# Encoder block on one core: the down projection becomes seven block products like the up projection, with its operands kept in DRAM

## The chip, the cores and the metric

The kernel runs on one NeuronCore of a Trainium2 chip. The metric is the device time of one execution in microseconds (us); lower is better. The engines are named as the profile names them: PE multiplies matrices (PEld is its weight load), DVE and ACT work elementwise, POOL does a little elementwise work at the very end, and SP issues the DMA transfers.

## What is computed

One layer of an encoder with 512 tokens and a model width of 2048; everything is float32. The change touches the last two lines of the block, the MLP:

```python
h = h + mixed @ w_out
hn = _rmsnorm(h, norm_mlp_w)
h = h + jnp.square(jax.nn.relu(hn @ w_mlp_up)) @ w_mlp_down
return _rmsnorm(h, norm_final_w)
```

`w_mlp_up` is 2048 x 8192 and `w_mlp_down` 8192 x 2048. Everything ahead of `w_out` (the input projection, neighbourhood attention, a gated delta rule, two projections) is the same in both kernels.

## The kernel before

Activations lie transposed, features on the 128 partitions and the 512 tokens along the row, so a 128-feature tile of `h` is 128x512. A float32 weight unit of 128x1024 (eight 128x128 blocks) is loaded in one 512 KB DMA and split in two: ACT rounds it to the PE's format (`wh`, the CAST of lines 89 and 94), DVE subtracts (`wl`, the TENSOR_TENSOR of lines 90 and 95). The right-hand operand is split the same way, and each block product takes three matmuls: high by high, high by low, low by high. `wh` and `wl` have three buffers each (line 87).

**Up projection (lines 841 to 964).** It runs as Winograd's form of Strassen's algorithm. A pair i of output tiles (`m0`, `m1`) and the two halves of the contraction give four weight units A11, A12, A21, A22; the tokens are cut in two halves of 256. Instead of eight products of a unit by a token half there are seven: A11, A12, A22 and the sums S1 to S4 of weight units, each against one of seven operands X11, X21, X22, T1 to T4 that are made once from `h` while `w_out` runs (lines 870 to 888). A product is 24 matmuls of 128x256 (lines 912 to 914), a pair 168, the 32 pairs 5376. A pair uses three PSUM banks a, b, c, and the results are gathered with copies and adds on ACT and DVE (lines 933 to 963): `t1`, `t5` and `u2` hold products between their uses. In program order, banks alternate: b is written by S2, then c by S1 and a by A12, then b again by S3, then c by S4, then b by A22. relu, the row scale `rB` and the square end in tiles `ur`, which are stored to `hidD` in DRAM (lines 959, 964), 64 tiles of 128x512.

**Down projection (lines 966 to 1028).** Plain: for each batch b of 2048 hidden features 16 tiles of `hidD` are reloaded (`hr`) and split whole (`hih`, `hil`, line 844). For each of the 16 output tiles two units of `w_mlp_down` are loaded and split, 48 matmuls of 128x512 run into one bank, and DVE adds the bank to `Ha`, which holds all of `h` in SBUF (line 983). Four batches make 62 such steps; the last two output tiles of the last batch run in token halves (64 times three matmuls of 128x256, lines 1016 to 1018), so that the final RMSNorm of the first half runs beside the matmuls of the second.

**What sets the order.** Each engine works through its own list in order; a scheduler sets these lists at build time. An instruction that waits holds everything behind it on its engine. `pump` (line 101) advances the RMSNorm statistics between matmuls.

Of the kernel before, what the change touches and what calls it, by code (L numbers as in the profile page):

```python
# [49 lines left out]
def tile_hybrid_block(  # L50
# [88 lines left out]
    def rstd_bcast(ps, sumsq, nm, cs=range(4), wait=0):  # L139
# [4 lines left out]
        dg = ev(f"dg_{nm}")  # L144
# [31 lines left out]
    hidD = dp.tile([64, 128, T], F32, name="hidD")  # L176
# [607 lines left out]
    with ExitStack() as p1:  # L784
# [56 lines left out]
        def load_hid(k):  # L841
            raw = ev(f"hr{k}")
            nc.sync.dma_start(out=raw, in_=hidD[k])
            return split(raw, big(f"hih{k}"), big(f"hil{k}"))
# [4 lines left out]
        def operand(src, name):  # L849
            t = bq.tile([128, T], F32R, tag="B2", name=name) if name.startswith("X11") else big(name)  # L850
            return split(src, t[:, 0:256], t[:, 256:512])

        lo_t, hi_t = slice(0, 256), slice(256, 512)
        XS = {}
        with ExitStack() as p5:
            tr = p5.enter_context(tc.tile_pool(name="tr", bufs=8, side="right", reuse_waits="tile"))
            TR = []
            xs = []
            for n, m in enumerate(m for j in range(8) for m in (j, j + 8)):
# [9 lines left out]
                xs.append(xr)  # L869
                if n % 2 == 0:  # L870
                    XS["11", m] = operand(xr[:, lo_t], f"X11_{m}")
                else:
                    j = n // 2
                    x0, x1 = xs[n - 1], xs[n]
                    XS["21", j] = operand(x1[:, lo_t], f"X21_{j}")
                    XS["22", j] = operand(x1[:, hi_t], f"X22_{j}")
                    t = tr.tile([128, 4, 256], F32, tag="tr", name=f"TR{j}")
                    V.tensor_tensor(out=t[:, 0], in0=x0[:, lo_t], in1=x0[:, hi_t], op=ALU.subtract)
                    V.scalar_tensor_tensor(out=t[:, 1], in0=t[:, 0], scalar=-1.0, in1=x1[:, hi_t], op0=ALU.mult, op1=ALU.subtract)
                    V.tensor_tensor(out=t[:, 2], in0=x1[:, hi_t], in1=x0[:, hi_t], op=ALU.subtract)  # L880
                    V.scalar_tensor_tensor(out=t[:, 3], in0=t[:, 1], scalar=-1.0, in1=x1[:, lo_t], op0=ALU.mult, op1=ALU.subtract)
                    TR.append(t)
            tasks.append(stat("h", sq))
            for o, e in (("T2", 1), ("T1", 0), ("T3", 2), ("T4", 3)):
                for j in range(8):
                    XS[o, j] = operand(TR[j][:, e], f"X{o}_{j}")

        with ExitStack() as p6:
            sm = p6.enter_context(tc.tile_pool(name="sm", bufs=1, side="right", reuse_waits="tile"))

            def load_a(src, name):
                raw = sm.tile([128, 1024], F32, tag="a", name=f"raw_{name}", bufs=2)
                nc.sync.dma_start(out=raw, in_=src)
                return raw

            def sums(name, bufs=4):
                return sm.tile([128, 1024], F32, tag="sum", name=name, bufs=bufs)

            def et(name):
                return sm.tile([128, 256], F32, tag="et", name=name, bufs=6)  # L900
# [6 lines left out]
            def product(ps, w, o, first=False):  # L907
                hi, lo = w
                for j in range(8):
                    rh, rl = XS[o, j]  # L910
                    c = slice(j * 128, (j + 1) * 128)
                    PE.matmul(ps, hi[:, c], rh, start=first and j == 0, stop=False, skip_group_check=True)  # L912
                    PE.matmul(ps, hi[:, c], rl, start=False, stop=False, skip_group_check=True)  # L913
                    PE.matmul(ps, lo[:, c], rh, start=False, stop=j == 7, skip_group_check=True)  # L914
                    if j % NPUMP == NPUMP - 1:
                        pump()

            for i in range(32):
                m0 = i // 8 * 16 + i % 8
                m1 = m0 + 8  # L920
                a11 = load_raw(wup[m0, 0], f"A11_{i}")
                a21 = load_a(wup[m1, 0], f"A21_{i}")
                a22 = load_raw(wup[m1, 1], f"A22_{i}")
                a12 = load_raw(wup[m0, 1], f"A12_{i}")
                s1, s3 = sums(f"S1_{i}"), sums(f"S3_{i}")
                V.tensor_tensor(out=s1, in0=a21, in1=a22, op=ALU.add)
                V.tensor_tensor(out=s3, in0=a21, in1=a11, op=ALU.add)
                a, b, c = (bank()[:, 0:256] for _ in range(3))
                t1, t5, u2 = et(f"t1_{i}"), et(f"t5_{i}"), et(f"u2_{i}")
                r0, r1 = ev(f"ur{m0}"), ev(f"ur{m1}")  # L930
                s2, s4 = sums(f"S2_{i}"), sums(f"S4_{i}")
                product(a, wsplit(a11, f"A11_{i}"), "11", True)
                S_.copy(out=t1, in_=a)
                V.tensor_tensor(out=s2, in0=s1, in1=a11, op=ALU.add)
                if i == 0:
                    V.tensor_tensor(out=s4, in0=s2, in1=a12, op=ALU.add)
                    product(c, wsplit(s4, f"S4_{i}"), "22", True)
                    S_.copy(out=t5, in_=c)
                    product(a, wsplit(a12, f"A12_{i}"), "21")
                product(b, wsplit(s2, f"S2_{i}"), "T2", True)  # L940
                V.tensor_tensor(out=u2, in0=b, in1=t1, op=ALU.add)
                product(c, wsplit(s1, f"S1_{i}"), "T1", i > 0)
                if i == 0:
                    V.tensor_tensor(out=t5, in0=c, in1=t5, op=ALU.subtract)
                else:
                    S_.copy(out=t5, in_=c)
                    product(a, wsplit(a12, f"A12_{i}"), "21")
                V.scalar_tensor_tensor(out=r0[:, lo_t], in0=a, scalar=0.0, in1=rB[:, lo_t], op0=ALU.max, op1=ALU.mult)
                product(b, wsplit(s3, f"S3_{i}"), "T3")
                V.tensor_tensor(out=t5, in0=b, in1=t5, op=ALU.add)  # L950
                V.tensor_tensor(out=t5, in0=t5, in1=t1, op=ALU.add)
                V.scalar_tensor_tensor(out=r1[:, hi_t], in0=t5, scalar=0.0, in1=rB[:, hi_t], op0=ALU.min, op1=ALU.mult)
                if i > 0:
                    V.tensor_tensor(out=s4, in0=s2, in1=a12, op=ALU.add)
                    product(c, wsplit(s4, f"S4_{i}"), "22")
# [31 lines left out]
        def finish(half, ts, sq):  # L987
# [4 lines left out]
            for m in range(16):  # L992
# [118 lines left out]
```

## Time and profile before

| | us |
|---|---|
| median of 3 runs (2923.11 to 2926.89) | 2926.62 |
| the profiled execution | 2922.42 |
| its span, first to last instruction | 2920.6 |
| PE busy in the span | 2850.9 |
| DVE busy | 1723.6 |
| ACT busy | 1017.2 |

The profiled execution is 4.2 us below the median. The mean granted clock of PE is 0.993 of full speed. In the page's 40 slices PE is busy over 90% in nearly all, so PE's list of matmuls is nearly the span, and a stage is read by the time between its first and last matmul. The stages that the change touches are the end of `w_out`, the up projection, which ends at 2199 us, and the down projection with the last norm.

### The profile page before, as it was taken

How to read it: one execution, taken by the hardware profiler on the slowest of the kernel's cores; microseconds unless marked ns; L12 is line 12 of the kernel's file. 1: busy time of each engine (PE TensorE's matmuls, PEld its weight loads, DVE VectorE, ACT ScalarE, POOL GpSimd, SP SyncE). 2: the span in 40 equal slices, each digit the busy share in tenths (PEclk: the TensorE clock that was granted, in tenths of full speed). 3: DMA queues.
4: the chain of work that ended last, by engine and by line, in shares of the span. 5: the costliest groups of instructions: out<-in, count | busy, mean ns of one | idle time of the engine just before them, and what ended most of it. 6: DMA issues, size and time to landing. Idle time of an engine off the chain costs nothing.

```text
span 2920.6 us, 39434 instructions
## 1 busy us (share of the span) xinstructions
PE 2850.9 (98%) x15736; PEld 2462.6 (84%) x15736; DVE 1723.6 (59%) x2592; ACT 1017.2 (35%) x1549; POOL 24.8 (1%) x66
## 2 busy tenths in 40 slices
PE   8999999999999999999996999999999999999998
PEld 6778788888788888888886999999997888888887
DVE  6888769744554444444448888888875242332333
ACT  6444322232333333222334444444444231222332
POOL 0000000000000000000000000000000000000000
PEclk9999999999999999999998999999999999999999
DMA  7655663655632323543433334333437343343332
GB/s 230 190 183 187 211 188 121 205 158 176 190 120 92 92 86 121 172 147 116 143 117 116 127 129 139 130 127 131 131 115 262 98 152 101 119 132 95 109 100 87
DMA packets 170874, 412.31 MB, mean 141 GB/s; under 512 B 34369, under 2 KB 46721, under 8 KB 170689
## 3 DMA queue, kind: packets, MB, share of 16 engines
q1 hardware_dynamic: 170016, 407.69, 43.8%
q0 software_dynamic: 672, 2.10, 0.3%
q8 instruction: 123, 2.02, 0.3%
q14 instruction: 63, 0.51, 0.1%
HBM read 350.84 MB, written 58.88 MB: 140 GB/s over the span
## 4 chain that ended last, share of the span: by engine, by line
PE 87%; DMA 6%; DVE 5%; issue 1%; ACT 1%; SPq 0%; DVEq 0%; ACTq 0%
PE ps_b L117 11%; PE ps_b L115 11%; PE ps_b L116 11%; PE ps_mm L115 9%; PE ps_mm L117 9%; PE ps_mm L116 9%; PE ps_b L912 7%; PE ps_b L913 7%; PE ps_b L914 7%; DMA bB<-rowD 1%; DMA Nd<-bB 1%; DVE wl_in L90 1%; DMA kb<-rowD 0%; DMA XQ<-Nd 0%; PE ps_ax L589 0%
## 5 line engine op out<-in xcount | busy, mean ns | idle before, releaser
L115 PE MATMUL ps_mm<-xh,wh_in 128*128 128x512 f32 x1416 | 565.9, 400 | 3.2 <-ACT wh_in L89 3.2
L117 PE MATMUL ps_mm<-xh,wl_in 128*128 128x512 f32 x1416 | 559.0, 395 | 0.7 <-DVE wl_in L90 0.7
L116 PE MATMUL ps_mm<-xl,wh_in 128*128 128x512 f32 x1416 | 558.5, 394 | 0.0
L115 PE MATMUL ps_b<-hih,wh_dn 128*128 128x512 f32 x992 | 386.6, 390 | 1.0 <-ACT hih L94 1.0
L117 PE MATMUL ps_b<-hih,wl_dn 128*128 128x512 f32 x992 | 386.0, 389 | 1.3 <-DVE wl_dn L90 1.3
L116 PE MATMUL ps_b<-hil,wh_dn 128*128 128x512 f32 x992 | 386.4, 390 | 0.0
L89 ACT CAST wh_in<-raw_in 128x1024 fp32r<-128x1024 f32 x177 | 186.0, 1051 | 408.7 <-PE ps_mm L116 331.8
L117 PEld LDWEIGHTS ps_mm<-xh,wl_in 128*128 128x128 f32 x1416 | 267.0, 189 | 60.8 <-DVE wl_in L90 1.6
L115 PEld LDWEIGHTS ps_mm<-xh,wh_in 128*128 128x128 f32 x1416 | 267.1, 189 | 58.4 <-ACT wh_in L89 3.6
L116 PEld LDWEIGHTS ps_mm<-xl,wh_in 128*128 128x128 f32 x1416 | 267.0, 189 | 54.8 <-issue 0.2
L89 ACT CAST wh_dn<-raw_dn 128x1024 fp32r<-128x1024 f32 x124 | 130.8, 1055 | 459.5 <-PE ps_b L116 446.5
L90 DVE TENSOR_TENSOR wl_dn<-raw_dn,wh_dn 128x1024 fp32r<-128x1024 f32 x124 | 151.9, 1225 | 230.3 <-ACT wh_dn L89 230.1
L90 DVE TENSOR_TENSOR wl_in<-raw_in,wh_in 128x1024 fp32r<-128x1024 f32 x177 | 216.0, 1221 | 119.8 <-ACT wh_in L89 110.2
L115 PEld LDWEIGHTS ps_b<-hih,wh_dn 128*128 128x128 f32 x992 | 186.2, 188 | 42.0 <-ACT hih L94 3.4
L116 PEld LDWEIGHTS ps_b<-hil,wh_dn 128*128 128x128 f32 x992 | 186.2, 188 | 40.9 <-DVE hil L95 2.3
L117 PEld LDWEIGHTS ps_b<-hih,wl_dn 128*128 128x128 f32 x992 | 186.2, 188 | 40.1 <-DVE wl_dn L90 2.1
L914 PE MATMUL ps_b<-XT,wl_S 128*128 128x256 f32 x768 | 217.3, 283 | 0.0
L913 PE MATMUL ps_b<-XT,wh_S 128*128 128x256 f32 x768 | 217.3, 283 | 0.0
L912 PE MATMUL ps_b<-XT,wh_S 128*128 128x256 f32 x768 | 217.2, 283 | 0.0
L94 ACT CAST wh_S<-S 128x1024 fp32r<-128x1024 f32 x128 | 134.1, 1048 | 211.7 <-PE ps_b L913 202.1
L95 DVE TENSOR_TENSOR wl_S<-S,wh_S 128x1024 fp32r<-128x1024 f32 x128 | 156.6, 1223 | 31.5 <-ACT wh_S L94 29.0
L983 DVE TENSOR_TENSOR Ha<-ps_b,Ha 128x512 f32<-128x512 f32 x62 | 42.9, 692 | 189.2 <-PE ps_b L117 189.2
(352 smaller groups left out, 5204.5 us busy)
## 6 DMA issues: line engine op xcount, KB each, us to landing
raw_in<-in_win SPq DMA_DIRECT2D x177, 512.0 KB
raw_A<-in_wup SPq DMA_DIRECT2D x128, 512.0 KB
raw_dn<-in_wdn SPq DMA_DIRECT2D x124, 512.0 KB
raw_wo<-in_wout SPq DMA_DIRECT2D x32, 512.0 KB
hidD<-ur SPq DMA_DIRECT2D x64, 256.0 KB
hr<-hidD SPq DMA_DIRECT2D x64, 256.0 KB
gD<-g SPq DMA_DIRECT2D x32, 256.0 KB
raw_pa<-in_wpa SPq DMA_DIRECT2D x16, 512.0 KB
```

The lines of the kernel that those rows point to most:

```text
L89: S_.copy(out=hi, in_=raw)
L90: V.tensor_tensor(out=lo, in0=raw, in1=hi.bitcast(F32), op=ALU.subtract)
L94: S_.copy(out=hi, in_=src)
L95: V.tensor_tensor(out=lo, in0=src, in1=hi.bitcast(F32), op=ALU.subtract)
L115: PE.matmul(ps, hi[:, w], rh, start=first and kk == 0, stop=False)
L116: PE.matmul(ps, hi[:, w], rl, start=False, stop=False)
L117: PE.matmul(ps, lo[:, w], rh, start=False, stop=last and kk == 7)
L912: PE.matmul(ps, hi[:, c], rh, start=first and j == 0, stop=False, skip_group_check=True)
L913: PE.matmul(ps, hi[:, c], rl, start=False, stop=False, skip_group_check=True)
L914: PE.matmul(ps, lo[:, c], rh, start=False, stop=j == 7, skip_group_check=True)
L983: V.tensor_tensor(out=H[m], in0=ps, in1=H[m], op=ALU.add)
```

## The change

Both projections now use one routine for the seven products. In the new order a pair goes Q4 (A22 by T4), P5 (S1 by T1), P1 (A11 by X11), P6 (S2 by T2), P7 (S3 by T3), P3 (S4 by X22), P2 (A12 by X21). Bank a takes Q4 and P2, bank c takes P5 and P3, and bank b takes P1, P6 and P7 directly after one another, P6 and P7 accumulating onto what is there; each partial sum is copied out in between (`tA`, `tB`).

The seven operands of the down projection are made from the hidden tiles at the end of each up pair, four more DVE operations, and stored to `hidD`, which is now [4 batches, 7 kinds, 128, 8, 256]. At each batch 28 loads of 256 KB bring them back through four buffers (`et`, which `tA` and `tB` use as well), and 56 splits of 128x256 fill them. `h` is no longer held in SBUF: each down pair loads its two tiles from `hTD` and stores them back, and twelve are reloaded at the end. Down work goes two pairs at a time, product by product in turn, as do the first and last two pairs of up. The first two up pairs start with P1 and P2, ahead of the splits of T1 to T4. The weight sums are made in place. The last two down pairs use another product order, and each half of the tokens is normed and stored by tiles of 128 KB.

The core of the diff (the up stage's old code and the last norm are cut):

```diff
-    hidD = dp.tile([64, 128, T], F32, name="hidD")
+    hidD = dp.tile([4, 7, 128, 8, 256], F32, name="hidD")
...
+            ROLE = {"P1": "11", "P2": "21", "P3": "22", "Q4": "T4", "P5": "T1", "P6": "T2", "P7": "T3"}
+            BANK = {"P1": "b", "P6": "b", "P7": "b", "P5": "c", "P3": "c", "Q4": "a", "P2": "a"}
+            FIRST = {"P1", "P5", "Q4", "P2"}
+            ORDER = ("Q4", "P5", "P1", "P6", "P7", "P3", "P2")
...
+                elif q == "P1":
+                    S_.copy(out=tA[:, 1], in_=ps)
+                elif q == "P6":
+                    S_.copy(out=tB[:, 1], in_=ps)
+                elif q == "P7":
+                    add(r1[:, hi_t], ps, tB[:, 0])
+                    add(r1[:, lo_t], ps, tA[:, 0])
+                    V.scalar_tensor_tensor(out=r1, in0=r1, scalar=0.0, in1=rB, op0=ALU.min, op1=ALU.mult)
+                    S_.activation(out=r1, in_=r1, func=AF.Square)
...
+                nc.sync.dma_start(out=hidD[b, 0, :, j, :], in_=r0[:, lo_t])
+                nc.sync.dma_start(out=hidD[b, 1:3, :, j, :].rearrange("o p t -> p o t"), in_=r1.rearrange("p (o t) -> p o t", o=2))
+                add(tA[:, 0], r0[:, lo_t], r0[:, hi_t], ALU.subtract)
+                V.scalar_tensor_tensor(out=tA[:, 1], in0=tA[:, 0], scalar=-1.0, in1=r1[:, hi_t], op0=ALU.mult, op1=ALU.subtract)
+                V.scalar_tensor_tensor(out=tB[:, 0], in0=tA[:, 1], scalar=-1.0, in1=r1[:, lo_t], op0=ALU.mult, op1=ALU.subtract)
+                add(r0[:, hi_t], r1[:, hi_t], r0[:, hi_t], ALU.subtract)
+                nc.sync.dma_start(out=hidD[b, 4:6, :, j, :].rearrange("o p t -> p o t"), in_=tA)
+                nc.sync.dma_start(out=hidD[b, 3, :, j, :], in_=tB[:, 0])
+                nc.sync.dma_start(out=hidD[b, 6, :, j, :], in_=r0[:, hi_t])
...
+            def a_tile(name):
+                return sm.tile([128, 1024], F32, tag="a", name=name, bufs=7)
+
+            def et(name):
+                return sm.tile([128, 2, 256], F32, tag="et", name=name, bufs=4)
...
+            up_group((0, 1), ("P1", "P2", "Q4", "P5", "P6", "P7", "P3"), first)
+            for i in range(2, 30):
+                up_group((i,), ORDER)
+            up_group((30, 31), ORDER)
+
+            NB = 4
+            def operands(b):
+                operand_tiles(OPS, f"h{b}_")
+                for o in ("T4", "T1", "11", "T2", "T3", "22", "21"):
+                    for j in range(0, 8, 2):
+                        raw = et(f"hr{b}{o}{j}")
+                        nc.sync.dma_start(out=raw, in_=hidD[b, OPS.index(o), :, j : j + 2, :])
+                        for e in range(2):
+                            fill(o, j + e, raw[:, e])
...
+                for q in order:
+                    for i, p in zip(idx, ps):
+                        t = run_product(p, q, a_tile)
+                        h0, h1 = p.h0, p.h1
+                        if q == "Q4":
+                            add(h1[:, lo_t], h1[:, lo_t], t, ALU.subtract)
...
+            for b in range(NB):
+                operands(b)
+                for g in range(0, 8, 2):
+                    if b < NB - 1 or g < 6:
+                        down_group(b, (g, g + 1), ORDER, lambda i, p, q, b=b: store(b, i, p, q))
...
+            down_group(NB - 1, (6, 7), ("Q4", "P1", "P6", "P7", "P2", "P5", "P3"), collect)
...
-                for u in range(2):
-                    unit_mm(ps, load_unit(wdn[m, 2 * b + u], f"dn{b}_{m}_{u}"), hid, 8 * u, u == 0, u == 1)
-                V.tensor_tensor(out=H[m], in0=ps, in1=H[m], op=ALU.add)
```

Three places show how the lists move. First PE in an up pair, number 10 of 32. Before, where one product gives way to the next (`ps_b` with its number is a bank; XT3_0 is block 0 of T3):

```order
L914 MATMUL ps_b_14542<-X21_7_12039,wl_A12_10_14641 128x256
L912 MATMUL ps_b_14543<-XT3_0_12098,wh_S3_10_14669 128x256
L913 MATMUL ps_b_14543<-XT3_0_12098,wh_S3_10_14669 128x256
L914 MATMUL ps_b_14543<-XT3_0_12098,wl_S3_10_14670 128x256
L912 MATMUL ps_b_14543<-XT3_1_12101,wh_S3_10_14669 128x256
```

The same pair after, at the hand-over of bank 14612 from P6 (S2) to P7 (S3):

```order
L904 MATMUL ps_b_14612<-XT2_x7_12069,wl_S2_u10_14640 128x256
L902 MATMUL ps_b_14582<-X22_x0_10855,wh_S4_u10_14702 128x256
L903 MATMUL ps_b_14582<-X22_x0_10855,wh_S4_u10_14702 128x256
L904 MATMUL ps_b_14582<-X22_x0_10855,wl_S4_u10_14703 128x256
L902 MATMUL ps_b_14582<-X22_x1_10856,wh_S4_u10_14702 128x256
L903 MATMUL ps_b_14582<-X22_x1_10856,wh_S4_u10_14702 128x256
L902 MATMUL ps_b_14612<-XT3_x0_12070,wh_S3_u10_14669 128x256
L903 MATMUL ps_b_14612<-XT3_x0_12070,wh_S3_u10_14669 128x256
```

Before, the bank of S3 was last written 48 matmuls earlier. Now five matmuls of S4 (11 in every second pair) stand between two products in one bank. Between P1 and P6 no other matmul stands. Then ACT at the same pair. Before:

```order
L94 CAST wh_A12_10_14640<-raw_A12_10_14536 128x1024
L933 COPY t1_10_14545<-ps_b_14542 128x256
L94 CAST wh_S3_10_14669<-S3_10_14539 128x1024
L94 CAST wh_S4_10_14701<-S4_10_14551 128x1024
L946 COPY t5_10_14546<-ps_b_14544 128x256
L94 CAST wh_A22_10_14733<-raw_A22_10_14534 128x1024
```

After:

```order
L94 CAST wh_S2_u10_14639<-A22_u10_14539 128x1024
L94 CAST wh_S3_u10_14669<-A21_u10_14540 128x1024
L979 COPY tA_u10_14572<-ps_b_14612 128x256
L94 CAST wh_S4_u10_14702<-A22_u10_14539 128x1024
L94 CAST wh_A12_u10_14731<-raw_A12_u10_14537 128x1024
L981 COPY tB_u10_14573<-ps_b_14612 128x256
```

The copy of line 981, which P7 waits for, stands behind the cast of A12, and this cast takes the `wh` buffer of S2, which P6 reads. Last, DVE at the change to batch 1 of the down projection. Before (`Ha` is `h`, dn1_11_0 a unit of batch 1):

```order
L90 TENSOR_TENSOR wl_dn1_11_0_21592<-raw_dn1_11_0_21589,wh_dn1_11_0_21591 128x1024
L90 TENSOR_TENSOR wl_dn1_11_1_21622<-raw_dn1_11_1_21619,wh_dn1_11_1_21621 128x1024
L983 TENSOR_TENSOR Ha_19801<-ps_b_21526,Ha_19801 128x512
L90 TENSOR_TENSOR wl_dn1_12_0_21654<-raw_dn1_12_0_21651,wh_dn1_12_0_21653 128x1024
L90 TENSOR_TENSOR wl_dn1_12_1_21684<-raw_dn1_12_1_21681,wh_dn1_12_1_21683 128x1024
```

After, from the split of S1 of the first pair (d1_0) to the weight sum A22 + A21 of the second (d1_1):

```order
L95 TENSOR_TENSOR wl_S1_d1_0_22061<-A22_d1_0_21979,wh_S1_d1_0_22060 128x1024
L95 TENSOR_TENSOR X22_h1_0_21767<-hr1220_21927,X22_h1_0_21767 128x256
L95 TENSOR_TENSOR X22_h1_1_21768<-hr1220_21927,X22_h1_1_21768 128x256
L95 TENSOR_TENSOR X22_h1_2_21769<-hr1222_21933,X22_h1_2_21769 128x256
L95 TENSOR_TENSOR X22_h1_3_21770<-hr1222_21933,X22_h1_3_21770 128x256
L95 TENSOR_TENSOR X22_h1_4_21771<-hr1224_21939,X22_h1_4_21771 128x256
L95 TENSOR_TENSOR X22_h1_5_21772<-hr1224_21939,X22_h1_5_21772 128x256
L95 TENSOR_TENSOR X22_h1_6_21773<-hr1226_21945,X22_h1_6_21773 128x256
L95 TENSOR_TENSOR X22_h1_7_21774<-hr1226_21945,X22_h1_7_21774 128x256
L909 TENSOR_TENSOR h1_3_21993<-h1_3_21993,ps_b_22033 128x256
L909 TENSOR_TENSOR A22_d1_1_21987<-A22_d1_1_21987,A21_d1_1_21988 128x1024
```

Eight splits of X22, and behind the last row shown the eight of X21, stand ahead of the second pair's S1 split, though their products come five and six places later in the order.

## Rows read from the trace of the kernel before

**Rows 1.** The page: busy time by engine; the chain that ended last by engine.

```profile
PE 2850.9 (98%) x15736; PEld 2462.6 (84%) x15736; DVE 1723.6 (59%) x2592; ACT 1017.2 (35%) x1549; POOL 24.8 (1%) x66
...
PE 87%; DMA 6%; DVE 5%; issue 1%; ACT 1%; SPq 0%; DVEq 0%; ACTq 0%
```

**Rows 2.** Windows, us: span, busy by engine (count), clock, DMA share, GB/s.

```profile
1535.00:1557.00 22.00, 1.65 (x5) 1.13 (x5) 17.23 (x39) 9.73 (x26) 0.00 (x0) 0.50 0.28 95
1557.00:1577.00 20.00, 20.00 (x157) 19.36 (x156) 16.48 (x20) 7.70 (x10) 0.00 (x0) 0.95 0.38 120
1600.00:1800.00 200.00, 200.00 (x1672) 200.00 (x1671) 167.22 (x200) 90.17 (x109) 0.00 (x0) 1.00 0.40 131
2195.00:2230.00 35.00, 33.27 (x154) 24.59 (x153) 19.79 (x28) 14.85 (x22) 0.00 (x0) 1.00 0.90 309
2300.00:2500.00 200.00, 200.00 (x884) 165.62 (x883) 67.52 (x72) 48.54 (x53) 0.00 (x0) 1.00 0.38 119
```

**Rows 3.** Groups, 1600:1800: line, engine, tiles, count, busy us, mean ns, idle.

```profile
L95 DVE TENSOR_TENSOR wl_S<-S,wh_S 128x1024 fp32r<-128x1024 f32 x40 | 48.9, 1223 | 9.4 <-ACT wh_S L94 8.6
...
L94 ACT CAST wh_S<-S 128x1024 fp32r<-128x1024 f32 x40 | 41.9, 1048 | 64.4 <-PE ps_b L913 64.4
...
L950 DVE TENSOR_TENSOR t<-ps_b,t 128x256 f32<-128x256 f32 x10 | 4.2, 425 | 6.9 <-PE ps_b L914 6.9
```

**Rows 4.** Timeline of DVE in the down projection: start, us, what [idle before].

```profile
2444.56 0.69 DVE L983 TENSOR_TENSOR Ha<-ps_b,Ha 128x512 f32<-128x512 f32 x1 [3.35 <-PE ps_b L117]
...
2455.44 0.69 DVE L983 TENSOR_TENSOR Ha<-ps_b,Ha 128x512 f32<-128x512 f32 x1 [3.35 <-PE ps_b L117]
```

**Rows 5.** Groups of the down projection, 2200:2920.

```profile
L983 DVE TENSOR_TENSOR Ha<-ps_b,Ha 128x512 f32<-128x512 f32 x62 | 42.9, 692 | 189.2 <-PE ps_b L117 189.2
...
L1018 PE MATMUL ps_b<-hih,wll 128*128 128x256 f32 x64 | 18.1, 283 | 0.0
```

**Rows 6.** Timeline, end of an up product and the add that reads it.

```profile
1696.14 0.28 PE L914 MATMUL ps_b<-XT,wl_A 128*128 128x256 f32 x1
...
1696.46 0.42 DVE L961 TENSOR_TENSOR t<-ps_b,t 128x256 f32<-128x256 f32 x1 [0.69 <-PE ps_b L914]
```

**Rows 7.** Timeline, an ACT cast and the copy behind it.

```profile
1699.23 1.05 ACT L94 CAST wh_A<-raw_A 128x1024 fp32r<-128x1024 f32 x1
...
1700.19 0.37 ACT L933 COPY t<-ps_b 128x256 f32<-128x256 f32 x1
```

**Rows 8.** Timeline, from w_out to the up projection.

```profile
1526.94 0.28 PE L912 MATMUL ps_b<-X,wh_A 128*128 128x256 f32 x1
...
1527.86 0.33 SPq L866 DMA_DIRECT2D hTD<-xr  x1
...
1529.94 0.72 ACT L868 ACTIVATE xr<-xr,nlw_s 128x512 f32<-128x512 f32 x1 [1.45 <-DMA hTD<-xr]
...
1535.03 10.81 DVE L95 TENSOR_TENSOR XT<-TR,XT 128x256 fp32r<-128x256 f32 x32
...
1545.87 6.31 SPq L893 DMA_DIRECT2D raw_A<-in_wup  x3
...
1555.35 0.58 PE L912 MATMUL ps_b<-X,wh_S 128*128 128x256 f32 x1 [23.61 <-ACT wh_S L94]
```

**Rows 9.** Waits of PE, 2195:2920.

```profile
PE ps_b L117 <- DVE wl_dn L90: 1.3, 2, 0.7
```

**Rows 10.** The chain in 2195:2222: start, us, what.

```profile
2202.17 4.37 DMA hr<-hidD
...
2207.94 3.38 DMA hr<-hidD
```

**Rows 11.** Timeline of PE where down begins, 2199:2202.

```profile
2199.42 0.39 PE L115 MATMUL ps_b<-hih,wh_dn 128*128 128x512 f32 x1
```

**Rows 12.** Timeline of the end, 2903:2921.

```profile
2904.29 0.41 DVE L1021 TENSOR_TENSOR Ha<-ps_b,Ha 128x256 f32<-128x256 f32 x1
...
2910.58 3.73 DVE L996 TENSOR_TENSOR Ha<-ps_b,Ha 128x256 f32<-128x256 f32 x11 [1.72 <-ACT rB L838]
```

More of the change, by code (lines that the diff above doesn't have):

```diff
@@ L868, in tile_hybrid_block @@
                 S_.activation(out=xr, in_=xr, func=AF.Copy, scale=nlw_s[:, m : m + 1])
[L869 removed]
+                j = n // 2
                 if n % 2 == 0:
[L871 to L882 removed]
@@ L883, in tile_hybrid_block @@
[L883 to L900, printed above, removed]
+                    x0 = xr
@@ L902, in wsplit, with load_a @@
+            operand_tiles(OPS[3:], "x")
+            early_fill = [(o, j) for o in OPS[3:] for j in range(8)]
+            tr_src = {(o, j): TR[o][:, j] for o, j in early_fill}
+            def load_a(pool_tile, src):
+                nc.sync.dma_start(out=pool_tile, in_=src)
+                return pool_tile
             def wsplit(raw, name):
@@ new lines, in open_pair, with run_product @@
+            def open_pair(nm, a11, a12):
+                p = Pair()
+                p.nm, p.ps, p.step = nm, {}, 0
+                p.a11, p.a12 = a11, a12
+                p.keep = False
+                return p
+            def run_product(p, q, sums):
+                nm = p.nm
+                if q == "Q4":
+                    w = wsplit(p.a22, f"A22_{nm}")
+                elif q == "P1":
+                    w = wsplit(p.a11, f"A11_{nm}")
+                elif q == "P2":
+                    w = wsplit(p.a12, f"A12_{nm}")
+                elif q == "P5":
+                    if not p.keep:
+                        add(p.a22, p.a22, p.a21)
+                    w = wsplit(p.a22, f"S1_{nm}")
+                elif q == "P6":
+                    if p.keep:
+                        add(p.a22, p.a22, p.a21)
+                        s2 = sums(f"S2_{nm}")
+                    else:
+                        s2 = p.a22
+                    add(s2, p.a22, p.a11)
+                    p.s2 = s2
+                    w = wsplit(s2, f"S2_{nm}")
+                elif q == "P7":
+                    add(p.a21, p.a21, p.a11)
+                    w = wsplit(p.a21, f"S3_{nm}")
+                else:
+                    add(p.s2, p.s2, p.a12)
+                    w = wsplit(p.s2, f"S4_{nm}")
+                bk = BANK[q]
+                if bk not in p.ps:
+                    p.ps[bk] = bank()[:, 0:256]
+                product(p.ps[bk], w, ROLE[q], q in FIRST)
+                return p.ps[bk]
@@ new lines, in tile_hybrid_block @@
+            first = [up_open(i) for i in range(2)]
+            heads = {}
+            for i, p in enumerate(first):
+                for q in ("P1", "P2"):
+                    heads[i, q] = wsplit(p.a11 if q == "P1" else p.a12, f"{q}_u{i}") if (i, q) in ((0, "P1"), (0, "P2"), (1, "P1")) else None
+            tasks.append(stat("h", sq))
+            for o, j in early_fill[:8]:
+                fill(o, j, tr_src[o, j])
+            for i, p in enumerate(first):
+                for q in ("P1", "P2"):
+                    w = heads[i, q] or wsplit(p.a12, f"{q}_u{i}")
+                    p.ps[BANK[q]] = bank()[:, 0:256]
+                    product(p.ps[BANK[q]], w, ROLE[q], True)
```

293 lines of the change are left out of this document (177 added, 116 removed).

## Prediction, written before the changed kernel ran

> **What bounds the kernel now.** The page comes first: PE is busy 98% of the span and makes 87% of the chain that ended last [rows 1], so time is won or lost only where PE's list gets shorter or stops. The windows by stage come next [rows 2]. In the up projection PE never rests at the full clock of 2.4 GHz, and DVE is busy 167.22 of 200 us: whatever is added to DVE there has little room. In the down projection PE is busy all the time too, with DVE at 67.52 of 200. The reader should see that the change makes PE's list shorter where DVE had room to spare, and that DVE takes its place. Groups, waits and the timeline then give the prices. A change of 0.2%, about 6 us, is what a measurement of this kernel can tell from none.
>
> **Matmuls of the down projection.** Before, a step of 48 wide matmuls takes 2455.44 - 2444.56 = 10.88 us [rows 4], and there are 62 steps [rows 5]: 674.6 us. The last two tiles take 3 x 64 = 192 matmuls of 256 columns [rows 5]. One of those costs 200 / 1672 = 0.1196 us [rows 2], so 23.0 us. Together 697.6. After, 32 pairs of 168 such matmuls make 5376 x 0.1196 = 643.0. That is **-54.6 us**. It is less than an eighth of 697.6, since two of the narrow matmuls cost 0.239 us and one wide one 0.227.
>
> **Waits of down before.** Down runs from 2199.42 [rows 11] to 2904.29 [rows 12], 704.9 us, 7.3 more than its matmuls. Only 1.3 of them stand in the longest row of PE's waits [rows 9], the rest is spread over the reload of the hidden tiles. They go with the old code: **-7.3**.
>
> **Start of up.** From 1526.94 to 2199.42 up takes 672.5 us [rows 8, 11] for 643.0 of matmul: 29.5 lost, of them 23.61 in one wait [rows 8]. The rows show it: 32 splits of T1 to T4 take DVE 10.81 us, then a weight load and the sums of weights until 1555.35 [rows 8]. After, P1 and P2 of two pairs, 96 matmuls, stand ahead of the need for T4, 72 more than before: 72 x 0.1196 = 8.6 us of work under the splits. The first product behind them is Q4, which takes A22 without a sum; before, sums and their split ran from about 1549.4 (1545.87 plus the load) to 1555.35, 5.9 us. Against it, the broadcast of `rB` stands between P2 of the first pair and P1 of the second and waits for a DVE operation behind the first eight splits; that wait lies beside the splits. I take 8.6 + 5.9 + 1 = **-15.5**, with -8 and -22 as ends (no sums saved; all but the load saved).
>
> **The 28 single pairs of up.** Here work is added to the path. P1, P6 and P7 accumulate in one bank one behind another, and each next product waits until ACT has copied the sum out. The trace of before shows no such wait, so I build it from rows. An add starts 0.32 us after the start of the last matmul of its product [rows 6]; a copy of 128x256 takes 0.37 [rows 7]. P1 to P6: 0.32 + 0.37 + some 0.05 for the signal, less the 0.12 after which the next matmul would have gone: 0.62 exposed, with nothing in between. P6 to P7: the copy stands behind the cast of A12, and this waits for P6 to give up a `wh` buffer, as casts of sums do now [rows 3]. Cast and copy stand 1700.19 - 1699.23 = 0.96 apart [rows 7]. So 0.16 + 0.96 + 0.37 + 0.05 - 0.12 = 1.42, of which five or eleven matmuls of S4 cover 0.60 or 1.32. On average 0.46 is left. With 0.12 for DVE, which at 17.5 us of work (16.7 now, from 167.22 in ten pairs, plus four small operations and two wider ones in the place of small ones) has little slack, the sum is 1.2 x 28 = **+34**. The ends are 0.62 x 28 = 17, if the second copy is hidden, and 2.04 x 28 = 57, if the pulled-up matmuls cover nothing. The rows of ACT's order decide for the middle.
>
> The Trainium skill, Perfetto Trace Analysis, section Matmuls, speaks against this: independent matmul groups should rotate through different PSUM banks, so that emptying one overlaps the next group. Taken by itself, the rule makes both hand-overs bubbles: +57 in place of +34.
>
> **Change from up to down.** The first loads of operands need buffers that `tA` and `tB` of pairs 30 and 31 hold until stored. After the last product of pair 30 come an add (0.42 [rows 3]), relu and square (0.7 and 0.6 as halves or wholes of such rows), and about three operations of 0.42, some 3 us; the store, 1529.94 - 1527.86 = 2.1 [rows 8]; the load, 4.37 [rows 10]; two splits, 0.7. That makes 10, of which pair 31's last product covers 2.9, and then DVE is short: a group of two pairs needs 22 operations of 1.22 [rows 3] and 16 of 0.42, 33.6 us, and the 56 splits of 10.81 / 32 = 0.34 add 18.9, 52.5 for 40.2 of matmul. So 7.5 + 12.3, **+20**. Ends: +8, if the splits find room in the groups around it; +35, if loads, at 0.90 DMA share already before [rows 2], fall behind as well.
>
> **Changes to batches 1 to 3.** The first tiles come free 5.7 us into the last group of a batch, and the last are needed 5.7 before the end of the next: 69 us, in which DVE has 33.6 x 69 / 40.2 + 18.9 = 76.6. That is 7.6 too much, and since eight splits of X22 and eight of X21 stand ahead of the second pair's S1, I take 8 each: **+24**. Ends 0 (the excess goes into slack of the groups beside) and 45 (15 each).
>
> **Clock.** Before the start of up PE was granted 0.50, its level of 1.2 GHz, during the long wait, and 0.95 in the 20 us after it, with 157 matmuls in place of 167 [rows 2]. That cost 10 x 0.12 = 1.2 us. The short waits in 2195:2230 did not lower it. For four changes I take 1.2 each: **+5**, between 0 and 10. The Trainium skill, TensorE: Matmul & The Clock Gate, last table, warns against idle gaps between bursts of matmuls, as they send the clock back to half; by that rule the term stands, by the row of 2195:2230 alone it would be 0.
>
> **End.** After the last product 2920.6 - 2904.29 = 16.3 us remain now. Then the squares of four tiles and more sums on PE lengthen the statistics, and sixteen output transfers a half take the place of four: **+3.5**, between 0 and 8. All other work keeps its cover: four more small DVE operations and five stores a pair lie beside matmuls, as do the loads and stores of `h`, at 0.38 to 0.40 of the DMA queues [rows 2]. If the DMA cover failed, it would show as waits of ACT for raw tiles.
>
> **Sum.** -54.6 - 7.3 - 15.5 + 34 + 20 + 24 + 5 + 3.5 = **+9**. Against the profiled execution of 2922.4 that is 2931.5, against the median, which lies 4.2 higher, 2935.5. I predict 2935.
>
> **Rivals.**
> - **It gets faster: cover is better than I walk.** If the second copy hides (17 for 34), the splits at the batch changes go into DVE's slack in the groups beside (0 to 8 for 24), and the first change costs its latency alone (8 to 12 for 20), the sum falls by 45, to -35: 2892. For it: in the down projection DVE has much room today [rows 2], and two interleaved pairs give each copy 2.9 us. Against: the order lists put the splits in front of the second pair's operands. It decides from the point where hand-overs, changes, clock and end together cost less than the 77.4 us gained (my walk has 86.5).
> - **DVE and loads fall further behind.** Both hand-overs exposed (57), 15 at each batch change (45), 30 at the first: +60, so 2985 at the worst; half of the way, +35, gives 2962. For it: the DMA share of 0.90 at the change [rows 2]. Against: DVE's excess, as worked out, is only 7.6.
> - **The start does not gain.** If the new head of up waits for its loads as the old one did, the -15.5 goes: +24, 2951. For it: the weight loads at 1545.87 also waited for the splits [rows 8]. Against: 8.6 us of matmuls are ready without them.
>
> **How the numbers follow.** The forecast has 0.40; of it 0.14 lies within 0.2% and 0.26 above. Faster has 0.30, of which 0.02 lies within 0.2%. The heavier loss has 0.20, all slower. The start without gain has 0.10, of which 0.04 lies within 0.2%, if other terms are kinder. So faster 0.28, same 0.20, slower 0.52. The range goes from 2898, which leaves out the lower half of the first rival, to 2964, which leaves out the worst of the second. The forecast's own range is 2924 to 2947.
>
> **What would show it.** In the profile after: up pairs 21.2 to 21.4 us apart in place of 20.1; PE waits at the first S2 matmul for the copy of line 979 (about 0.6 each) and at the first S3 matmul for that of line 981; a group of down at 40.2 us in mid-batch without waits; PE waits for DVE's `wl` or operand tiles of some 8 us at each batch change and 20 at the first; a wait of about 10 at the start in place of 23.6. I am wrong if up pairs keep 20.1, or if groups at a change keep 40.

## The result and the profile after

| | before | after |
|---|---|---|
| median, us | 2926.7 (2923.1 to 2926.9, 4 runs) | 2955.6 (2953.1 to 2963.2, 4 runs) |
| profiled execution | 2922.4 | 2953.1 |
| span | 2920.6 | 2951.3 |

The changed kernel is slower: 1.0106 of the time of before, 95% interval 1.0086 to 1.0126, or +28.9 us between the medians. The forecast was +9, or 2935, with a range of 2898 to 2964 and a range of its own of 2924 to 2947.

The page of the changed kernel, busy time and the chain by engine, answers to [rows 1]:

```profile
PE 2831.7 (96%) x17944; PEld 2547.0 (86%) x17944; DVE 2070.7 (70%) x3195; ACT 1167.5 (40%) x1869; POOL 24.8 (1%) x66
...
PE 76%; DVE 9%; DMA 8%; ACT 3%; issue 2%; SPq 0%; DVEq 0%; ACTq 0%
```

PE is busy 19 us less than before in a span that is 31 us longer: it has less work and stands more. DVE has 347 us more to do. Where PE stands is told by its waits from 1520 us to the end (waiting matmul <- releaser: us in total, times, longest):

```profile
PE ps_b L902 <- ACT wh_S_d L94: 16.2, 6, 3.5
PE ps_b L902 <- ACT tA_u L979: 13.5, 28, 1.0
PE ps_b L902 <- ACT wh_A_d L94: 9.8, 3, 3.7
PE ps_b L902 <- ACT XT_h L94: 9.1, 2, 8.3
PE ps_b L904 <- DVE wl_S_u L95: 8.4, 13, 0.7
PE ps_b L904 <- DVE wl_A_d L95: 8.1, 4, 2.7
```

Names with `_u` belong to up, with `_d` and `_h` to down. There are two kinds: 28 small waits for the copy of line 979, one for each single pair of up, with 13 for a `wl` beside them; and a few long ones in down. The windows (columns as in [rows 2]) show the stages:

```profile
1600.00:1800.00 200.00, 193.16 (x1573) 189.38 (x1572) 158.20 (x198) 89.84 (x122) 0.00 (x0) 1.00 0.45 138
2219.00:2229.00 10.00, 1.74 (x11) 1.26 (x9) 10.00 (x17) 2.90 (x5) 0.00 (x0) 0.71 0.58 168
...
2410.00:2415.00 5.00, 2.32 (x17) 2.11 (x17) 4.25 (x11) 3.07 (x7) 0.00 (x0) 0.93 0.84 257
2425.00:2430.00 5.00, 3.21 (x13) 2.92 (x14) 4.97 (x8) 2.53 (x4) 0.00 (x0) 0.50 0.76 280
2380.00:2445.00 65.00, 56.29 (x436) 55.38 (x435) 57.24 (x101) 34.62 (x66) 0.00 (x0) 0.92 0.68 224
2440.00:2480.00 40.00, 40.00 (x336) 40.00 (x335) 33.98 (x40) 14.69 (x14) 0.00 (x0) 1.00 0.52 170
```

Up ran 1672 matmuls in 200 us before [rows 2], now 1573 in the same 200. In mid-batch, 2440:2480, down runs without a gap. The change to batch 1 lies in 2380:2445: 436 matmuls, at 0.1196 us each 52.1 of 65 us, so 12.9 lost. All losses below are counted in this way, time less 0.1196 for each matmul, summed over the stretch in which matmuls come late.

| part (profiled executions, us) | forecast | measured |
|---|---|---|
| matmuls of down | -54.6 | -54.6 |
| waits of the old down | -7.3 | -7.3 |
| start of up | -15.5 | -16.9 |
| 28 single pairs | +34 | +38.8 |
| change from up to down | +20 | +26.3, of them waits 17.7 |
| changes to batches 1 to 3 | +24 | +40.0, of them waits 26.7 |
| clock | +5 | in the two rows above: about 15 of the 21.9 that are not wait |
| end | +3.5 | +2.6 |

The rows for the matmuls and the waits of the old down are worked out by count and price, the others are read from the trace. Ahead of the change the profiled execution of after was 1.5 us quicker, and 3.3 us of the span's 30.7 are in no row (delays under 0.05 us each, and the rounding of 0.1196 over 10,700 matmuls).

### The profile page after: what moved, and what is told of

Read it like the earlier page. It is cut to its first block, busy times and chain, and to the rows that moved or that the text cites. A ratio compares the mean times of both kernels' runs of the same rounds, so it can differ in the third digit from the quotient of the medians.

```text
span 2951.3 us, 45595 instructions
## 1 busy us (share of the span) xinstructions
PE 2831.7 (96%) x17944; PEld 2547.0 (86%) x17944; DVE 2070.7 (70%) x3195; ACT 1167.5 (40%) x1869; POOL 24.8 (1%) x66
## 4 chain that ended last, share of the span: by engine, by line
PE 76%; DVE 9%; DMA 8%; ACT 3%; issue 2%; SPq 0%; DVEq 0%; ACTq 0%
PE ps_b L902 12%; PE ps_b L904 11%; PE ps_b L903 11%; PE ps_mm L116 8%; PE ps_mm L115 8%; PE ps_mm L117 8%; PE ps_b L115 4%; PE ps_b L117 4%; PE ps_b L116 4%; DMA hr<-hidD 2%; ACT wh_S_u L94 1%; DMA bB<-rowD 1%; DMA Nd<-bB 1%; DVE wl_S_u L95 1%; DVE A_u L909 1%
## 5 line engine op out<-in xcount | busy, mean ns | idle before, releaser
L902 PE MATMUL ps_b<-XT_x,wh_S_u 128*128 128x256 f32 x768 | 223.2, 291 | 13.7 <-ACT tA_u L979 13.5
L902 PE MATMUL ps_b<-XT_h,wh_S_d 128*128 128x256 f32 x768 | 221.1, 288 | 12.6 <-ACT wh_S_d L94 12.6
L904 PE MATMUL ps_b<-XT_h,wl_S_d 128*128 128x256 f32 x768 | 221.0, 288 | 0.8 <-DVE wl_S_d L95 0.8
L903 PE MATMUL ps_b<-XT_h,wh_S_d 128*128 128x256 f32 x768 | 220.9, 288 | 0.0
L904 PE MATMUL ps_b<-XT_x,wl_S_u 128*128 128x256 f32 x768 | 217.6, 283 | 0.0
L903 PE MATMUL ps_b<-XT_x,wh_S_u 128*128 128x256 f32 x768 | 217.6, 283 | 0.0
L95 DVE TENSOR_TENSOR wl_S_u<-A_u,wh_S_u 128x1024 fp32r<-128x1024 f32 x128 | 155.0, 1223 | 47.9 <-ACT wh_S_u L94 47.8
L95 DVE TENSOR_TENSOR wl_S_d<-A_d,wh_S_d 128x1024 fp32r<-128x1024 f32 x124 | 151.6, 1223 | 21.9 <-ACT wh_S_d L94 21.0
L902 PEld LDWEIGHTS ps_b<-XT_x,wh_S_u 128*128 128x128 f32 x768 | 147.1, 192 | 22.7 <-ACT tA_u L979 19.2
L902 PEld LDWEIGHTS ps_b<-XT_h,wh_S_d 128*128 128x128 f32 x768 | 151.1, 197 | 13.4 <-ACT wh_S_d L94 13.4
L902 PE MATMUL ps_b<-X_h,wh_A_d 128*128 128x256 f32 x512 | 146.6, 286 | 10.3 <-ACT wh_A_d L94 9.8
L904 PEld LDWEIGHTS ps_b<-XT_h,wl_S_d 128*128 128x128 f32 x768 | 151.2, 197 | 1.0 <-DVE wl_S_d L95 1.0
```

The lines of the kernel that those rows point to most:

```text
L95: V.tensor_tensor(out=lo, in0=src, in1=hi.bitcast(F32), op=ALU.subtract)
L902: PE.matmul(ps, hi[:, c], t[:, lo_t], start=first and j == 0, stop=False, skip_group_check=True)
L903: PE.matmul(ps, hi[:, c], t[:, hi_t], start=False, stop=False, skip_group_check=True)
L904: PE.matmul(ps, lo[:, c], t[:, lo_t], start=False, stop=j == 7, skip_group_check=True)
```

## Experiments

Ratios are to runs of the kernel before on the same chip. Losses by run, in us, from the profiled execution; "up pair" is the distance of two single pairs of up. In code that no edit touches, up starts at 1525.4 us in the changed kernel's profile and at up to 1534.7 in those of the experiments (e3), so the losses, which count from up on, price an edit more closely than the difference of two medians.

| run | median, us | of before (95%) | up pair | first change | batch change, mean |
|---|---|---|---|---|---|
| changed kernel | 2955.6 | 1.0106 (1.0086 to 1.0126) | 21.5 | 26.3 | 13.3 |
| e1, up order | 2925.0 | 0.9989 (0.9979 to 1.0000) | 20.1 | 26.5 | 14.1 |
| e2, late splits | 2945.9 | 1.0062 (1.0047 to 1.0077) | 21.5 | 26.7 | 8.3 |
| e3, no reload | 2915.1 | 0.9957 (0.9940 to 0.9974) | 21.5 | 27.0 | 0.0 |
| e4, half the subtractions on POOL | 2941.7 | 1.0049 (1.0034 to 1.0064) | 21.5 | 21.2 | 9.9 |
| e5, e1 + e2 + e4 | 2911.5 | 0.9937 (0.9919 to 0.9955) | 20.1 | 21.7 | 9.7 |
| e6, e1 + e2 + buffers | 2899.0 | 0.9898 (0.9884 to 0.9913) | 20.1 | 14.7 | 9.3 |
| e7, e1 + e2 + e4 + buffers | 2899.3 | 0.9898 (0.9881 to 0.9914) | 20.1 | 14.8 | 8.9 |
| e8, buffers alone | 2943.5 | 1.0049 (1.0034 to 1.0064) | 21.5 | 16.8 | 11.8 |
| e9, no subtraction | 2921.6, one run | | 21.5 | 27.0 | 0.4 |
| e10, no loads | 2952.5, one run | | 21.5 | 31.8 | 8.9 |

### e1: another order of products in up

```diff
+            UP_ORDER = ("Q4", "P1", "P5", "P6", "P3", "P7", "P2")
...
-                up_group((i,), ORDER)
+                up_group((i,), UP_ORDER)
```

> Only the order of the seven products in the 28 single up pairs changes, to Q4, P1, P5, P6, P3, P7, P2, so that two products in one PSUM bank always have another product of 2.9 us between them. Theory of the hand-over: the 36.9 us that PE loses between 1603 and 2172 us in the changed kernel come from the copies between P1, P6 and P7 in one bank; the waits for the copies go, pairs come 20.1 to 20.4 us apart, and the time falls by 33 to 38 us, to about 2919. Rival, DVE is the bound of a pair (158 of 200 us busy, and its list lengthened by four small operations): the waits for the copies turn into waits for wl, pairs stay at 21 us or more, and the time falls by less than 12 us.

What is at stake stands in the changed kernel's timeline at one pair, first between P1 and P6, then between P6 and P7 (start, us, what [idle before]):

```profile
1629.48 0.28 PE L904 MATMUL ps_b<-X_x,wl_A_u 128*128 128x256 f32 x1
1629.80 0.37 ACT L979 COPY tA_u<-ps_b 128x256 f32<-128x256 f32 x1 [0.59 <-PE ps_b L904]
...
1630.22 0.39 PE L902 MATMUL ps_b<-XT_x,wh_S_u 128*128 128x256 f32 x1 [0.46 <-ACT tA_u L979]
```

```profile
1633.32 1.04 ACT L94 CAST wh_A_u<-raw_A_u 128x1024 fp32r<-128x1024 f32 x1 [0.39 <-PE ps_b L903]
...
1634.25 0.39 PE L904 MATMUL ps_b<-X_x,wl_S_u 128*128 128x256 f32 x1 [0.65 <-DVE wl_S_u L95]
1634.27 0.37 ACT L981 COPY tB_u<-ps_b 128x256 f32<-128x256 f32 x1
```

The copy starts 0.32 us after the start of the last matmul of P1 and takes 0.37, and S2's first matmul goes 0.74 after that start, where it would have gone 0.12 after: 0.62, as worked out from [rows 6, 7]. At P6 to P7 the copy stands behind the cast of A12 by 0.95, as forecast, but PE doesn't even get through the five matmuls that cover it, since the third needs a `wl_S` that DVE makes late.

Measured: 2925.0, or 30.7 us below the changed kernel, a little less than the 33 to 38 expected. In the traces up itself, from its first matmul to its last, takes 658.5 us in place of 694.3, or 35.8 less. The same 200 us of up in e1:

```profile
1600.00:1800.00 200.00, 200.00 (x1672) 200.00 (x1671) 169.63 (x210) 95.52 (x130) 0.00 (x0) 1.00 0.47 151
```

PE is full again, with 1672 matmuls as before, though DVE does more than in [rows 2] (169.63 against 167.22). So up's loss was the hand-over in one bank and not DVE's work: the theory holds, the rival falls. Alone, this order makes the changed kernel as fast as the one before.

### e2: operands split shortly before their use

```diff
-                for o in ("T4", "T1", "11", "T2", "T3", "22", "21"):
+                for o in KINDS[:2]:
+                    operand_fill(b, o)
...
-                for q in order:
+                for n, q in enumerate(order):
+                    if idx[0] == 0 and n + 2 < 7:
+                        operand_fill(b, KINDS[n + 2])
```

> Only the place of the operand splits moves: each kind of operand is loaded and split two products ahead of its use in the first group of a batch, in place of all seven kinds ahead of that group. Work and transfers are the same. Theory of order: at a batch change the weight casts and splits of the next product stand in ACT's and DVE's lists behind splits that are needed four to six products later and that wait for their loads; the three changes lose 13.3 us each now and would lose under 6 each, so the time falls by 20 to 30 us. Rival, amount of work on DVE (7.6 us too much at each change): the same work remains, the time stays within 8 us. Rival, loads (four buffers, DMA share 0.8 to 0.9): the loads also start later, the stalls stay or grow.

Measured: 9.7 us less by the medians; a batch change loses 8.3 in place of 13.3, or 15 for the three. That is between the theories. ACT still runs into loads, and a weight cast stands behind:

```profile
2420.47 0.40 ACT L94 CAST XT_h<-hr1T 128x256 fp32r<-128x256 f32 x1 [4.42 <-DMA hr1T<-hidD]
2420.78 1.04 ACT L94 CAST wh_S_d<-A_d 128x1024 fp32r<-128x1024 f32 x1
```

Order is worth 5 us at a change, and something else holds the other 8.

### e3: no reload at batches 1 to 3

```diff
-                operands(b)
+                if b == 0:
+                    operands(b)
```

> Leaves out part of the computation: the operands of batches 1 to 3 of the down projection are neither reloaded nor split, all batches multiply those of batch 0. It prices the three batch changes as a whole. If stalls and the half clock behind them all come from reloading, the three changes lose under 1 us each in place of 13.3, and the time falls by 38 to 41 us, to about 2916. If weight loads or the interleaved groups themselves cost something there, less goes.

Measured: 40.5 us less, and the window of the first of the three changes is without a gap:

```profile
2380.00:2445.00 65.00, 65.00 (x545) 65.00 (x544) 52.15 (x62) 23.88 (x23) 0.00 (x0) 1.00 0.45 141
```

So all of the 40 us belong to reloading. Interleaved groups and weight loads cost nothing there.

### e4: every second subtraction on POOL

```diff
-                            fill(o, j + e, raw[:, e])
+                            t = XS[o, j + e]
+                            S_.copy(out=t[:, lo_t], in_=raw[:, e])
+                            eng = G if e else V
+                            eng.tensor_tensor(out=t[:, hi_t], in0=raw[:, e], in1=t[:, lo_t].bitcast(F32), op=ALU.subtract)
```

> Of each two operand splits in the down projection one subtraction moves from DVE to POOL, which takes 0.73 us for one of 128x256 in the norm at the end. It takes 28 x 0.34 = 9.5 us from DVE at each of the four changes and leaves order, casts and loads as they are. Theory of the amount of work on DVE: the excess of 7.6 us is gone, and each change loses 4 us or less where it loses 13.3 (26 at the first): the time falls by 30 us or more. Theory of order and loads: PE waits for casts that stand behind casts that wait for loads, and DVE has idle time between them; the time falls by less than 12 us.

Measured: 13.9 us less, 9.9 a batch change and 21.2 at the first: neither theory's number. The experiment didn't do what it was made for. Groups of DVE in 2385:2440, in e4:

```profile
L95 DVE TENSOR_TENSOR wl_S_d<-A_d,wh_S_d 128x1024 fp32r<-128x1024 f32 x10 | 12.9, 1301 | 1.2 <-ACT wh_S_d L94 1.2
...
L1068 DVE TENSOR_TENSOR X_h<-hr,X_h 128x256 fp32r<-128x256 f32 x12 | 8.4, 714 | 1.0 <-ACT X_h L1066 1.0
```

and in the changed kernel in the same stretch:

```profile
L95 DVE TENSOR_TENSOR wl_S_d<-A_d,wh_S_d 128x1024 fp32r<-128x1024 f32 x9 | 11.0, 1221 | 1.3 <-ACT wh_S_d L94 1.2
...
L95 DVE TENSOR_TENSOR X_h<-hr,X_h 128x256 fp32r<-128x256 f32 x24 | 8.9, 419 | 1.1 <-ACT X_h L94 1.0
```

Half the splits took DVE nearly the same time (8.4 us for 12, 8.9 for 24): beside POOL's work a split on DVE takes 714 ns on average in place of 419. DVE was busy 59.73 of 65 us at the change, against 57.24 without POOL's help. So e4 says nothing against DVE's work as the cause.

### e5, e6, e7, e8: combinations and buffers

e8 changes only numbers of buffers (`hr` tiles come from `et`):

```diff
-                return sm.tile([128, 1024], F32, tag="a", name=name, bufs=7)
+                return sm.tile([128, 1024], F32, tag="a", name=name, bufs=6)
...
-                return sm.tile([128, 2, 256], F32, tag="et", name=name, bufs=4)
+                return sm.tile([128, 2, 256], F32, tag="et", name=name, bufs=7)
```

In e6 and e7 `et` keeps four, and operand loads have three of their own, which serve all of T4 and T1 at the first change:

```diff
+            def hr_tile(b, o, j):
+                n = KINDS.index(o) * 4 + j // 2
+                if b == 0 and n < 8 or n % 7 < 3:
+                    return sm.tile([128, 2, 256], F32, tag="hr", name=f"hr{b}{o}{j}", bufs=3)
+                return et(f"hr{b}{o}{j}")
```

> Puts three edits together: the product order of e1 in the single up pairs, the late splits of e2 and the subtractions on POOL of e4. If order and work are separate causes at a batch change, the 13.3 us fall by 5 (e2) and 3.4 (e4) to about 5 each and the first change by 5 to about 21: 24 for the changes and 31 for up, so about 2901. If what is left at a change is the loads (ACT's casts wait for them in either order), the two edits overlap: 8 us each at the batch changes, about 2910.

> The product order of e1, the late splits of e2, and three buffers of their own for operand loads beside the four shared ones (for that, the weight-sum tiles have six buffers in place of seven). Theory of loads: at the first change T4 is loaded before up ends, its wait of 8 to 10 us goes and the 26 us become 12 or less; at the batch changes ACT's waits for loads of up to 4.4 us go and the 8 us become 4 or less: about 2900. Theory of work on DVE: the first change keeps 15 or more, the others 7 to 8: 2910 or more. A lost weight buffer could cost something everywhere; it would show as waits for weight tiles in mid-batch.

> All edits of e5 and e6 together. If work on DVE and waits for loads are both causes, it is the fastest, 5 to 15 us below the better of the two, at 2885 to 2895; if only one of them is, it equals the better one within 4 us.

> The changed kernel with seven shared buffers for up's copies and operand loads in place of four, and six for weight sums in place of seven; order and work are unchanged. Theory of loads: three more buffers halve ACT's waits for operand loads at a batch change (15.5 us now); the changes lose 8 us or less in place of 13.3, the first 18 or less in place of 26, and the time falls by 15 to 25 us. Theory of order and work: the casts of the next weights stand behind the same splits, and the time falls by less than 8 us.

Measured: at the first change the buffers are what counts. 26.3 falls to 16.8 with them alone and to 14.7 with the late splits; the wait of 8.3 us at the first matmul of down is gone, since loads of T4 no longer stand behind the stores of `tA` and `tB`. At the batch changes they do little: 11.8 alone, 9.3 in e6 against 8.3 in e2. At the batch changes POOL adds nothing to either (e5, e7); at the first it takes off 5 us (e4, e5), but not on top of the buffers (e7 against e6). The expected 4 or 5 us a batch change came in none of the four. e5 met the second of its times, 2910, in which the two edits overlap; e7 equals e6, as expected if only one of the two causes is left; e8 saved 12.1, between its theories. e6 met its time of about 2900, but not by its parts, 12 or less at the first change and 4 or less at the others. It takes 2899.0 where the kernel of before took 2928.4 on the same chip, a ratio of 0.9898 (0.9884 to 0.9913): with e7, which equals it, it beats both kernels. What it still loses, in windows at the first change and at that to batch 1:

```profile
2180.00:2260.00 80.00, 69.25 (x547) 68.38 (x546) 71.38 (x116) 38.44 (x66) 0.00 (x0) 0.91 0.72 232
2340.00:2405.00 65.00, 60.56 (x474) 59.48 (x474) 58.93 (x105) 33.87 (x62) 0.00 (x0) 0.95 0.71 233
```

### e9 and e10: the work without the loads, and the loads without the work

e9 keeps loads and casts of batches 1 to 3 and leaves out DVE's part; e10 keeps the splits and lets them read one loaded tile:

```diff
                         for e in range(2):
-                            fill(o, j + e, raw[:, e])
+                            if b == 0:
+                                fill(o, j + e, raw[:, e])
+                            else:
+                                S_.copy(out=XS[o, j + e][:, lo_t], in_=raw[:, e])
```

```diff
-                        raw = et(f"hr{b}{o}{j}")
-                        nc.sync.dma_start(out=raw, in_=hidD[b, OPS.index(o), :, j : j + 2, :])
+                        if b == 0 or n == 0 and j == 0:
+                            raw = et(f"hr{b}{o}{j}")
+                            nc.sync.dma_start(out=raw, in_=hidD[b, OPS.index(o), :, j : j + 2, :])
```

> Leaves out part of the computation: at batches 1 to 3 the operands' low halves are not made anew, so their 56 subtractions on DVE a batch go; all loads, casts and lists otherwise stay. Theory of work on DVE (19 us of splits in 69 us that have room for 12): each of the three changes loses under 3 us in place of 13.3, and the time falls by 30 us or more from the changed kernel's 2955. Theory of loads and order: ACT's casts still wait for loads and weight casts stand behind them; each change keeps 8 us or more.

> Leaves out part of the computation: at batches 1 to 3 one load of 256 KB stands for all 28, and all 56 splits of a batch read that tile. Work on ACT and DVE stays, the transfers go. Theory of work on DVE: each of the three changes keeps 7 us or more. Theory of loads: each loses under 4 us in place of 13.3, and the time falls by 28 us or more from 2955.

The same window, in e9:

```profile
2380.00:2445.00 65.00, 64.78 (x541) 64.57 (x540) 49.49 (x62) 39.57 (x74) 0.00 (x0) 1.00 0.78 257
```

and in e10:

```profile
2380.00:2445.00 65.00, 58.64 (x475) 58.44 (x474) 64.46 (x112) 37.34 (x76) 0.00 (x0) 0.95 0.38 126
```

With every load and cast in place, at 0.78 of the DMA queues, the changes cost 0.4 us each once DVE's 56 subtractions are out. (Its load buffers also come free sooner, since only the cast reads them; for the loads themselves there is e10.) Without the loads DVE is busy 64.46 of 65 us, and each change still loses 8.9, most of it in one wait:

```profile
PE ps_b L904 <- DVE wl_A_d L95: 6.4, 1, 6.4
```

So DVE's work is the cause at the batch changes. Loads and list order add to it only by leaving DVE idle while it has too much to do (57.24 of 65 busy in the changed kernel): 13.3 less 8.9 is 4.4 us, and e2 gets back about as much, 5.0. Two things stay open. No run joins the late splits of e2 to e10's missing loads, so that it is not shown how much of the 8.9 is the amount of DVE's work and how much its place in DVE's list; that DVE is busy for nearly the whole window speaks for the amount. And e10, of which there is one run, loses 31.8 at the first change, which its edit leaves alone.

## Why the prediction was right, and what was mis-sized

The direction was right, and every term had its sign. The size was a third of what came, +9 for +28.9. The 2955.6 measured lie outside the forecast's own range of 2924 to 2947; they lie in the wide one only because it also takes in half of the heavier loss, so that the hit of the number is in part luck. These are the terms.

- **Matmuls, old waits, start, end.** Right within 1.4 us each. At the start 96 matmuls of P1 and P2 do run beside the splits, and PE waits 4.1 us for `rB`'s broadcast as the list said; that is its longest wait there, where the sign named one of about 10.
- **Single pairs.** "1.2 x 28" was 1.39 x 28, of which 1.9 us in the first of these pairs stay in e1. The first hand-over was exact at 0.62, with 0.10 behind it that I left out: after such a wait the next matmul, too, comes 0.1 us late. The second was taken as 0.46 plus 0.12 for DVE; together they measured 0.67 on average. The wait stands, where five matmuls were pulled up, inside those five, for a `wl_S`, and not at S3's first matmul as forecast. With the 35.8 us that up gains in e1, the place of the products is nearly all there is to it. The rule of the Trainium skill that was weighed there (Perfetto Trace Analysis, section Matmuls: groups should rotate through PSUM banks) named the fault; its extreme, +57, was too dear, since part of the second hand-over was covered.
- **Batch changes.** "7.6 too much" for DVE is what e9 and e10 show: without the loads 8.9 are lost, 6.4 of them in the wait, without the subtractions 0.4. Waits in the changed kernel were 26.7 us for three changes, against 24. Two of the three at a change (shown below) end with a cast on ACT, where the forecast had DVE's `wl` or operand tiles. At the first of the two DVE is behind it all the same, since the weight sum that the cast reads is made late, behind the splits of X22; at the second the cast stands behind operand casts that wait for loads:

```profile
2420.64 1.22 DVE L909 TENSOR_TENSOR A_d<-A_d,A_d 128x1024 f32<-128x1024 f32 x1
2421.97 1.05 ACT L94 CAST wh_S_d<-A_d 128x1024 fp32r<-128x1024 f32 x1
...
2424.93 0.71 ACT L94 CAST X_h<-hr 128x256 fp32r<-128x256 f32 x2 [0.69 <-DMA hr<-hidD]
2425.55 1.99 ACT L94 CAST wh_A_d<-raw_A_d 128x1024 fp32r<-128x1024 f32 x2
```

- **First change.** Waits of 17.7 against 20. Of the two parts, the latency through the shared buffers (7.5 forecast, 8.3 waited) is shown by e6 and e8, in which it goes; that the rest is DVE's excess was argued, not tried apart.
- **Clock: the step that failed.** "For four changes I take 1.2 each" came from the one wait before up. Measured are 26.3 - 17.7 = 8.6 at the first change and 40.0 - 26.7 = 13.3 at the other three, 21.9 for 5. Not all of it is the clock. A wait costs more than its idle time at the full clock too: in the rows under e1, 0.46 idle lost 0.72. Counted matmul by matmul, such extras make about 6.5 of the 21.9, a cost that the forecast put at nothing, and about 15 are matmuls that follow one another without a pause, but 0.21 us apart in place of 0.12.

  The 1.2 was too small even for one pause, since in e10 a single wait of 6.4 loses 8.9. It came from a window that opens 1.65 us after PE had started again, and some seven of the ten matmuls missing in it are the room of a broadcast matmul of line 149, which holds PE until 1557.87. Besides, I had one long pause in mind, but DVE's excess comes out as several. PE's waits at the change to batch 1 are three:

```profile
2413.01 0.39 PE L904 MATMUL ps_b<-XT_h,wl_A_d 128*128 128x256 f32 x1 [2.68 <-DVE wl_A_d L95]
...
2423.06 0.39 PE L902 MATMUL ps_b<-XT_h,wh_S_d 128*128 128x256 f32 x1 [2.81 <-ACT wh_S_d L94]
...
2426.64 0.58 PE L902 MATMUL ps_b<-X_h,wh_A_d 128*128 128x256 f32 x1 [3.07 <-ACT wh_A_d L94]
```

  Matmuls run slower for a while after the first and after the third; after the second only two run before PE stops again. Behind the first, in 2414.5:2417.5, the granted clock is 0.50, the level of 1.2 GHz, and 16 matmuls take 3.00 us, where the full clock does them in 1.9; it is 0.50 in 2425:2430 too:

```profile
2414.50:2417.50 3.00, 3.00 (x16) 3.00 (x15) 3.00 (x8) 1.40 (x5) 0.00 (x0) 0.50 0.74 231
```

  The row of 2195:2230 [rows 2], from which short waits seemed to cost no clock, had pauses of at most 0.7 us [rows 9]. By the rule of the Trainium skill, TensorE: Matmul & The Clock Gate, section Why this matters for your kernels, idle gaps between bursts bring the clock back to half; the trace agrees with it at 0.50.

Of the rivals, the third (the start does not gain, 2951) comes nearest to the time and has no part in it, since the start gained 16.9. The second (DVE and loads fall behind, half of the way at 2962) is the next, but by another mechanism: hand-overs and waits were near the forecast, and what follows a wait, the clock above all, made most of the rest. (Its worst case of +60 is +63 by its own terms.) The first one's cover (splits in the slack of the groups beside) did not come, since the lists put far splits first and DVE was short in sum.

## What to carry to other kernels

Where sums accumulate in one PSUM bank with copies between them, put another bank's product between any two: here an order of seven names was worth 31 us by the medians. Before operands go through memory again, sum up the work of the engine that unpacks them over the stretch in which buffers are free and needed, here 76.6 us in 69; what is too much there comes back as waits, and with late splits and more buffers 8 to 9 us a change still stayed (e2, e6). And price a wait with what follows it: here 44.4 us of waits at the changes brought 21.9 more, about 15 of them by the slow clock.

## What was not expected of the hardware

- POOL and DVE slow each other. With POOL subtracting beside it, a DVE split of 128x256 took 714 ns on average in place of 419 and one of 128x1024 1301 in place of 1221. POOL itself took 984 to 1080 ns for one of 128x256, where a multiplication of that size takes it 730 in the final norm of the kernel before; these are two different operations (e4, then the kernel before):

```profile
L1068 POOL TENSOR_TENSOR XT_h<-hr1T,XT_h 128x256 fp32r<-128x256 f32 x12 | 12.7, 1080 | 13.2 <-ACT XT_h L1066 13.2
...
L994 POOL TENSOR_TENSOR Ha<-Ha,rB 128x256 f32<-128x256 f32 x10 | 7.0, 730 | 1796.1 <-ACT rB L838 1796.1
```

  The Trainium skill, Perfetto Trace Analysis, section Optimizing Scalar/DVE Operations, says that the two share an SBUF read port, so that moving work between them might not help. These rows agree.
- A single short pause of PE was enough for the lower clock. In the changed kernel PE stood 2.68 us until 2413.01, after a stretch without a pause, and the granted clock of 2414.5:2417.5 was 0.50. In 1600:1800, where it stood at most 0.7 us at a time, the clock was 1.00.
